# A decoder step on one Trainium2 core: the last two row tiles of the output projections multiplied together, and the rows behind them transposed in two halves

## The chip, the core and the metric

The kernel runs on one core of a Trainium2 chip. A core has TensorE for matmuls (PE in the profile), VectorE (DVE), ScalarE (ACT), GpSimd (POOL), SyncE (SP, which issues most transfers) and 16 DMA engines. Each engine takes its own instructions in order and waits for the others through semaphores. The metric is the device time of one execution in microseconds; lower is better.

## The reference

One layer of a decoder for a prompt of 1024 rows and for a group of 8 sample rows, all in float32. Only this part of it bears on the change:

```python
xp = xp + merge_heads(fox_prompt(q, k, v, logf), sgu_prompt(u, z, w_s[l], b_s[l]),
                      g_att_out[l], g_sgu_out[l], w_o[l])        # ... @ w_o, 1024 x 1024
...
xp = xp + cross_attend(rmsnorm(xp, g_cross[l]), mk, mv, w_cq[l], w_co[l])
f, conv_p = conv_ffn(rmsnorm(xp, g_ffn[l]), zeros, w_up[l], conv_w[l], conv_b[l], w_down[l])
xp = xp + f

def rmsnorm(x, g):
    return x * rsqrt(mean(x * x, axis=-1) + EPS) * g
def cross_attend(xn, mk, mv, w_cq, w_co):
    q = (xn @ w_cq)...   # then softmax over 256 memory rows
    return o @ w_co
```

So there are two output projections (w_o and w_co). Behind each stands a residual add, a norm of the sum, and a projection of the normed rows (w_cq, and the up projection of the feed-forward part). The sample rows go through the same layer, with attention over 8192 cached keys and values each, read page by page from a paged cache.

## The kernel before, in words

The prompt is worked in two halves of 512 rows, and a half is four tiles of 128 rows (tiles 0 to 3). Products of float32 are made in three terms: each operand is split into a high part in a short float format and a remainder, and one 128-row slice of the contraction takes three matmuls, high by high, high by low and low by high (`gemm3`, L270 to L272). The split of an operand is one pass on ACT (the high part, L236, or L233 for weights) and one on DVE (the remainder, L237, or L234). A contraction of 1024 has 8 slices, so one output tile of 128x512 takes 24 matmuls.

`out_proj` is called four times: for w_o and for w_co in each half. It works the 1024 output columns in two parts. In the first (n = 0) all four row tiles are multiplied slice by slice together. In the second (n = 1) the tiles are multiplied one after the other, 24 matmuls each, and each is followed by `residual` (L960 adds the product to the rows in place on DVE; L228 squares and sums them on ACT). Tile 3's residual of the second part is put in at high priority. Where the feed-forward part follows (w_co, `ys` given), the rows are also scaled by their norm factor: `factor` (L976 on ACT, then a power on POOL, L977) and `scaled` (L983 on ACT), tile 3's in two halves of 512 columns and only once the transposing has got to it.

`norm_T` stands behind each `out_proj`: behind w_o at the head of `cross`, behind w_co at the head of `ffn`. It turns the rows around by matmuls against the identity (transposes), splits them, and feeds the first output tile of the next projection as they come (`first`). It takes tiles 0 to 2 together first: eight PSUM banks with three transposes each (L1035), a split of 384 columns each, then 24 matmuls of 384 columns. Tile 3 follows: 8 transposes (L1051), eight splits of 128 columns, 24 matmuls of 128 columns. The other output tiles of the next projection take all 512 columns at once and come behind that.

The places of this text are numbered by time: place 1 is w_o and the cross norm of the first half, place 2 w_co and the feed-forward norm of the first half, places 3 and 4 the same of the second half.

The sample rows run as a background: a generator whose steps are put between those of the prompt at a given pace and which `held[0]` stops from the end of an `out_proj` to the end of the `norm_T` behind it. Its DVE work is large passes over cache pages: L1346 (keys times query) and L1350 (sum), some 1.2 us each for 128x1024. What is issued here is then ordered for each engine by a scheduler that plans with estimated durations and priorities; an engine follows its list in order. PSUM has four banks of pool `ba` and two of `bb` that the products and the transposes share. The split weights have five buffers for the high part (`wh`) and four for the remainder (`wl`).

## Time and profile before

| what | value |
|---|---|
| median of 3 runs | 1874.36 us (1873.6 to 1876.26) |
| profiled execution, its own time | 1871.72 us |
| its span in the trace | 1870.0 us |
| granted TensorE clock, mean | 0.983 |
| PE / DVE / ACT / POOL busy | 95% / 74% / 40% / 27% |

The busy share says which engine carries the span; the chain of work that ended last says who was waited for, step by step. In a table of windows each engine has its busy time and the count of its instructions in the stretch, then the clock that TensorE was granted (1.00 is full), the busy share of the DMA engines and the rate. A row of the timeline has the start, the duration, engine, line, operation and tiles, and in square brackets how long the engine had been idle and for whom it waited. A row of the waits has the waiting engine, line and tile, who released it, the total, the count and the longest. The duration of one matmul includes its way through the array, so matmuls overlap: how fast they follow each other is read from their starts.

### The profile page before, as it was taken

The numbers are of one execution on the slowest core, as the hardware profiler recorded it, in microseconds if no ns is written. First come the engines' busy times: TensorE is split into PE (matmuls) and PEld (weight loads), VectorE is DVE, ScalarE is ACT, GpSimd is POOL, SyncE is SP. The second block draws the span as 40 slices with busy tenths as digits, with TensorE's granted clock in tenths as the row PEclk, the third lists the DMA queues.
The fourth block names the chain that finished last, engine by engine and source line by source line (L and its number), as shares of the span: only waits on it lengthen the run. The fifth ranks groups of instructions, "written<-read, shape, count | busy, mean of one in ns | idle before, by whom it ended". The sixth has DMA issues, their size and how long they took to land.

```text
span 1870.0 us, 24215 instructions
## 1 busy us (share of the span) xinstructions
PE 1785.5 (95%) x9239; PEld 1296.8 (69%) x9239; DVE 1391.7 (74%) x1664; ACT 749.3 (40%) x1363; POOL 497.9 (27%) x437
## 2 busy tenths in 40 slices
PE   8999998788998999999999999989899999999998
PEld 5987666556676767776777776766576668767775
DVE  4889568776778787889989899898875549754344
ACT  6332355565633445433323234234354333333232
POOL 1232352241121322214233242343222112111110
PEclk9999999998999999999999999999999999999999
DMA  8877889684596867668878789888787678578972
GB/s 316 295 260 274 312 303 325 226 247 141 193 396 230 336 244 289 240 245 328 313 264 314 286 316 357 351 305 339 294 306 288 253 258 287 172 264 270 346 287 80
DMA packets 157012, 521.27 MB, mean 279 GB/s; under 512 B 20808, under 2 KB 40520, under 8 KB 124128
## 3 DMA queue, kind: packets, MB, share of 16 engines
q0 software_dynamic: 57168, 341.14, 49.0%
q1 hardware_dynamic: 92816, 165.99, 25.5%
q10 hardware_dynamic: 6912, 12.59, 1.8%
q8 instruction: 73, 1.20, 0.3%
q14 instruction: 43, 0.35, 0.0%
HBM read 495.73 MB, written 23.93 MB: 278 GB/s over the span
## 4 chain that ended last, share of the span: by engine, by line
PE 72%; issue 9%; DVE 7%; DMA 6%; ACT 3%; POOL 3%; SPq 0%; POOLq 0%; DVEq 0%; ACTq 0%
PE ba L270 11%; PE ba L272 11%; PE ba L271 10%; PE bb L270 6%; PE bb L271 6%; PE bb L272 6%; PE dv L1405 5%; DMA kv<-cache_k,kidx 3%; DVE s L1350 2%; DMA kv<-cache_v,kidx 1%; DVE kv L1346 1%; PE ba L1001 1%; PE dv L1669 1%; PE ba L1002 1%; PE ba L1003 1%
## 5 line engine op out<-in xcount | busy, mean ns | idle before, releaser
L233 ACT ACTIVATE wh<-wr 128x1024 fp32r<-128x1024 f32 (+2 forms) x220 | 228.6, 1044 | 501.6 <-PE ba L271 159.7
L234 DVE TENSOR_TENSOR wl<-wr,wh 128x1024 fp32r<-128x1024 f32 (+2 forms) x220 | 262.6, 1201 | 154.0 <-PE ba L272 58.2
L1340 POOL DMA_INDIRECT kv<-cache_k,kidx x128 | 198.5, 1551 | 616.8 <-DVE s L1350 403.9
L1346 DVE TENSOR_TENSOR kv<-kv,d 128x1024 f32<-128x1024 f32 (+1 forms) x184 | 295.5, 1635 | 37.1 <-DMA kv<-cache_k,kidx 28.0
L1350 DVE TENSOR_REDUCE s<-kv 128x16 f32<-128x1024 f32 (+1 forms) x184 | 296.6, 1627 | 0.1
L1399 POOL DMA_INDIRECT kv<-cache_v,kidx x128 | 173.7, 1357 | 294.0 <-PE dv L1405 216.8
L270 PE MATMUL ba<-wh,u 128*128 128x512 f32 (+1 forms) x601 | 229.3, 383 | 5.6 <-DVE u L960 2.7
L271 PE MATMUL ba<-wl,u 128*128 128x512 f32 (+1 forms) x601 | 228.1, 380 | 0.0
L272 PE MATMUL ba<-wh,u 128*128 128x512 f32 (+1 forms) x601 | 225.1, 380 | 0.0
L271 PE MATMUL ba<-u,wh 128*128 128x512 f32 (+2 forms) x520 | 202.7, 390 | 1.3 <-DVE u L237 1.3
L270 PE MATMUL ba<-u,wh 128*128 128x512 f32 (+2 forms) x520 | 202.3, 391 | 0.0
L272 PE MATMUL ba<-u,wl 128*128 128x512 f32 (+2 forms) x520 | 201.9, 389 | 0.0
L270 PEld LDWEIGHTS ba<-wh,u 128*128 128x128 f32 x601 | 113.2, 189 | 36.8 <-issue 8.0
L270 PE MATMUL bb<-u,wh 128*128 128x512 f32 (+2 forms) x344 | 136.6, 397 | 0.0
L1405 PE MATMUL dv<-kv,s 128*32 128x512 f32 x1024 | 131.2, 617 | 5.3 <-DMA kv<-cache_v,kidx 5.3
L271 PE MATMUL bb<-u,wh 128*128 128x512 f32 (+2 forms) x344 | 136.0, 395 | 0.2 <-DVE u L237 0.2
L272 PE MATMUL bb<-u,wl 128*128 128x512 f32 (+2 forms) x344 | 135.3, 394 | 0.0
L272 PEld LDWEIGHTS ba<-wh,u 128*128 128x128 f32 x601 | 113.0, 188 | 27.5 <-issue 6.1
L271 PEld LDWEIGHTS ba<-wl,u 128*128 128x128 f32 x601 | 113.3, 189 | 25.6 <-issue 4.8
L271 PEld LDWEIGHTS ba<-u,wh 128*128 128x128 f32 x520 | 98.6, 190 | 29.7 <-issue 7.2
L272 PEld LDWEIGHTS ba<-u,wl 128*128 128x128 f32 x520 | 98.2, 189 | 27.4 <-issue 7.6
L270 PEld LDWEIGHTS ba<-u,wh 128*128 128x128 f32 x520 | 98.2, 189 | 25.1 <-issue 4.6
(427 smaller groups left out, 3040.8 us busy)
## 6 DMA issues: line engine op xcount, KB each, us to landing
wr<-w_up SPq DMA_DIRECT2D x88, 512.0 KB
kv<-w_up POOLq DMA_DIRECT2D x22, 1024.0 KB, 7.8
wr<-w_down SPq DMA_DIRECT2D x40, 512.0 KB
kv<-w_down POOLq DMA_DIRECT2D x11, 1024.0 KB, 6.2
wr<-w_in SPq DMA_DIRECT2D x16, 512.0 KB
wr<-w_o SPq DMA_DIRECT2D x16, 512.0 KB
wr<-w_cq SPq DMA_DIRECT2D x16, 512.0 KB
wr<-w_co SPq DMA_DIRECT2D x16, 512.0 KB
```

What stands on the lines that cost most here:

```text
L233: nc.scalar.activation(h, src, AF.Copy)
L234: nc.vector.tensor_tensor(l, src, h.bitcast(F32), op=ALU.subtract)
L270: mmul(out, sh, mh, start=(i == 0), stop=False)
L271: mmul(out, sh, ml, start=False, stop=False)
L272: mmul(out, sl, mh, start=False, stop=(i == n - 1))
L1001: mmul(pss[i], mh[k][:, tb], wh, start=(k == korder[0]), stop=False)
L1002: mmul(pss[i], mh[k][:, tb], wl, start=False, stop=False)
L1340: nc.gpsimd.indirect_dma_start(kv, None, a["cache_k"], off(kidx[:, b, ch : ch + 1]))
L1346: nc.vector.tensor_tensor(kvv[:, i : i + m, :], kvv[:, i : i + m, :], qb.unsqueeze(1).broadcast_to((P, m, 512)), op=ALU.mult)
L1350: nc.vector.tensor_reduce(s[:, ch * 4 + i : ch * 4 + i + m, :].rearrange("p k h -> p (k h)"), kvv[:, i : i + m, :].rearrange("p k (h d) -> ...
L1399: nc.gpsimd.indirect_dma_start(kv, None, a["cache_v"], off(kidx[:, b, ch : ch + 1]))
L1405: mmul(dv[32 * j : 32 * j + 32, :], s[:, ch * 4 : ch * 4 + 4, :].rearrange("p k h -> p (k h)"), kvv[:, j, :], start=(ch == 1), stop=(ch == ...
```

## The change

In the second column part of `out_proj`, tiles 0 and 1 are multiplied as before, and tiles 2 and 3 as a pair: each slice of the weights is used for both before the next. The residuals of both tiles then follow the pair, both at high priority. With `ys`, tiles 0 and 1 are scaled at full width, and tiles 2 and 3 later, in alternating halves of 512 columns (`both`). `norm_T` takes tiles 0 and 1 first and then tiles 2 and 3, with the same code: for each half four PSUM banks of four transposes, eight splits of 256 columns, and 24 matmuls of 256 columns.

```diff
@@ residual @@
-        with tc.high_priority() if HP and i == 3 and n == 1 else nullcontext():
+        with tc.high_priority() if HP and i > 1 and n == 1 else nullcontext():
@@ out_proj @@
         def scaled(i, r):
             y = U([P, D])
-            for c in (slice(0, 512), slice(512, D)) if i == 3 else (slice(0, D),):
-                nc.scalar.activation(y[:, c], xt[i][:, c], AF.Copy, scale=r)
+            nc.scalar.activation(y, xt[i], AF.Copy, scale=r)
             return y
+        def both(r2, r3):
+            y2, y3 = U([P, D]), U([P, D])
+            for c in (slice(0, 512), slice(512, D)):
+                nc.scalar.activation(y2[:, c], xt[2][:, c], AF.Copy, scale=r2)
+                nc.scalar.activation(y3[:, c], xt[3][:, c], AF.Copy, scale=r3)
+            return [y2, y3]
...
-            for i in range(4):          # n == 1: one tile, gemm3 over 8 slices, then its residual
-                    ps = MM()
-                    gemm3(ps[:, :512], [... for k in korder])
-                if ys is not None and n == 1 and i > 0:
-                    ys.append(scaled(i - 1, factor(i - 1)))
-                residual(xt, sq, i, n, ps)
-                held[0] = n == 1 and i == 3
-                yield 5.2 if n else 0.1
+            for group in ((0,), (1,), (2, 3)):
+                pss = [MM() for _ in group]
+                for k in korder:
+                    wh, wl = (ws[k // 2][q][:, k % 2, :] for q in range(2))
+                    for i, ps in zip(group, pss):
+                        tb = slice(i * P, (i + 1) * P)
+                        mmul(ps, mh[k][:, tb], wh, start=(k == korder[0]), stop=False)
+                        mmul(ps, mh[k][:, tb], wl, start=False, stop=False)
+                        mmul(ps, ml[k][:, tb], wh, start=False, stop=(k == korder[-1]))
+                    if len(group) == 2 and k == korder[3]:
+                        yield 5.2
+                if ys is not None and group[0]:
+                    ys.append(scaled(group[0] - 1, factor(group[0] - 1)))
+                for i, ps in zip(group, pss):
+                    residual(xt, sq, i, n, ps)
+                held[0] = len(group) == 2
+                yield 5.2
         if ys is not None:
             with tc.high_priority():
-                ys.append(partial(scaled, 3, factor(3)))
+                ys.append(partial(both, factor(2), factor(3)))
@@ norm_T @@
-        for kk in range(8):             # tiles 0 to 2: 3 transposes, split of 384
-            ...
-        first(hs, ls, slice(0, 384))
-        yield 4
-        for k4 in range(0, 8, 4):       # tile 3: 4 transposes a bank, splits of 128
-            ...
-        first(hs, ls, slice(384, 512))
+        for t0 in (0, 2):
+            c = slice(t0 * P, (t0 + 2) * P)
+            if callable(ys[t0]):
+                ys[t0:] = ys[t0]()
+            for kk in range(0, 8, 2):
+                ...
+                tr = TR()               # 2 slices x 2 tiles = 4 transposes
+                ...
+                for q in range(2):
+                    k = kk + q
+                    split(tr[:, q * 256 : (q + 1) * 256], hs[k][:, c], ls[k][:, c], scale=gp[:, g0 + k : g0 + k + 1])
+                yield 0.6
+            first(hs, ls, c)
+            if t0 == 0:
+                yield 3
```

Up to the first second-part product of w_o the order of every engine is the same. PE has 6942 rows before and 6946 now, DVE 1491 and 1484, ACT 1169 and 1171; POOL (442) and SP (408) keep their counts. Lines behind the edit move by 14 (the key passes L1346 and L1350 are L1360 and L1364 after it).

On PE at place 1, before, tile 3's product (into `ba_4974`, the row tiles' slices are `u`) ends and the transposes (L1035) of tiles 0, 1 and 2 begin:

```order
L272 MATMUL ba_4974<-wh_4858,u_4631 128x512
L270 MATMUL ba_4974<-wh_4858,u_4630 128x512
L271 MATMUL ba_4974<-wl_4857,u_4630 128x512
L272 MATMUL ba_4974<-wh_4858,u_4631 128x512
L1035 MATMUL ba_5035<-cp,u_4678 128x128
L1035 MATMUL ba_5035<-cp,u_4680 128x128
L1035 MATMUL ba_5035<-cp,u_4682 128x128
L1035 MATMUL ba_5043<-cp,u_4678 128x128
```

Now, with tiles 2 and 3 in `ba_4931` and `ba_4932` taking turns at each slice and the transposes being L1059:

```order
L1028 MATMUL ba_4932<-wh_4858,u_4631 128x512
L1026 MATMUL ba_4931<-wh_4858,u_4630 128x512
L1027 MATMUL ba_4931<-wl_4857,u_4630 128x512
L1028 MATMUL ba_4931<-wh_4858,u_4631 128x512
L1026 MATMUL ba_4932<-wh_4858,u_4630 128x512
L1027 MATMUL ba_4932<-wl_4857,u_4630 128x512
L1028 MATMUL ba_4932<-wh_4858,u_4631 128x512
L1059 MATMUL ba_5037<-cp,u_4678 128x128
L1059 MATMUL ba_5037<-cp,u_4680 128x128
L1059 MATMUL ba_5037<-cp,u_4678 128x128
L1059 MATMUL ba_5037<-cp,u_4680 128x128
```

The transposes that follow the product read tiles 0 and 1 (`u_4678`, `u_4680`) alone.

On DVE at the same place, before, from tile 1's residual (L960) to the first remainder of the transposed rows (L237); `wl` are the remainders of w_cq's slices, L1346 and L1350 the background:

```order
L960 TENSOR_TENSOR u_4680<-bb_4903,u_4680 128x512
L960 TENSOR_TENSOR u_4682<-ba_4931,u_4682 128x512
L1332 TENSOR_TENSOR dec_4968<-ms_4965,d_1004_4806 128x512
L234 TENSOR_TENSOR wl_5012<-wr_5010,wh_5013 128x1024
L1346 TENSOR_TENSOR kv_4959<-kv_4959,d_388_2409 128x1024 x2
L234 TENSOR_TENSOR wl_5018<-wr_5016,wh_5019 128x1024
L1350 TENSOR_REDUCE s_2411<-kv_4959 128x16
L234 TENSOR_TENSOR wl_5024<-wr_5022,wh_5025 128x1024
L1350 TENSOR_REDUCE s_2411<-kv_4959 128x16
L234 TENSOR_TENSOR wl_5030<-wr_5028,wh_5031 128x1024
L960 TENSOR_TENSOR u_4684<-ba_4974,u_4684 128x512
L237 SCALAR_TENSOR_TENSOR u_5040<-ba_5035,gp,u_5039 128x384
```

Now (L1346 is what L1332 was, L1360 and L1364 the key passes):

```order
L960 TENSOR_TENSOR u_4680<-bb_4903,u_4680 128x512
L234 TENSOR_TENSOR wl_5012<-wr_5010,wh_5013 128x1024
L234 TENSOR_TENSOR wl_5018<-wr_5016,wh_5019 128x1024
L1346 TENSOR_TENSOR dec_4966<-ms_4963,d_1004_4806 128x512
L1360 TENSOR_TENSOR kv_4957<-kv_4957,d_388_2409 128x1024 x2
L234 TENSOR_TENSOR wl_5024<-wr_5022,wh_5025 128x1024
L1364 TENSOR_REDUCE s_2411<-kv_4957 128x16 x2
L960 TENSOR_TENSOR u_4682<-ba_4931,u_4682 128x512
L234 TENSOR_TENSOR wl_5030<-wr_5028,wh_5031 128x1024
L960 TENSOR_TENSOR u_4684<-ba_4932,u_4684 128x512
L237 SCALAR_TENSOR_TENSOR u_5036<-ba_5037,gp,u_5035 128x256
```

Tile 2's residual has moved behind three of the four `wl` passes and both key passes, tile 3's stays last, and two `wl` passes have moved to the front.

On ACT at place 2, before, behind the last weight split there, to the first high part of tile 3 (L236 high parts, L228 squares, L976 factors, L983 scaling; `u_4684` is tile 3):

```order
L236 ACTIVATE u_6251<-ba_6255,gp 128x384
L236 ACTIVATE u_6265<-ba_6269,gp 128x384
L228 ACTIVATE junk_6208,sqx_5831<-u_4684 128x512
L236 ACTIVATE u_6265<-bb_6261,gp 128x384
L976 ACTIVATE fac_1272_6210<-sqx_5831,part_5832 128x1
L228 ACTIVATE junk_6213,ssu_5054<-u_5740 128x512
L228 ACTIVATE junk_6215,ssu_5054<-u_5740 128x512
L236 ACTIVATE u_6279<-ba_6275,gp 128x384
L236 ACTIVATE u_6279<-bb_6283,gp 128x384
L983 ACTIVATE u_6289<-u_4684,fac_1272_6210 128x512 x2
L236 ACTIVATE u_6237<-ba_6316,gp 128x128
```

Now, from tile 2's factor to the first high part of the second half (L989 and L990 scale tiles 2 and 3, `u_4682` and `u_4684`):

```order
L976 ACTIVATE fac_1268_6203<-sqx_5829,part_5830 128x1
L228 ACTIVATE junk_6201,sqx_5829<-u_4684 128x512
L236 ACTIVATE u_6229<-bb_6231,gp 128x256
L236 ACTIVATE u_6240<-ba_6242,gp 128x256
L976 ACTIVATE fac_1269_6206<-sqx_5829,part_5830 128x1
L228 ACTIVATE junk_6209,ssu_5051<-u_5738 128x512
L236 ACTIVATE u_6251<-ba_6253,gp 128x256
L989 ACTIVATE u_6297<-u_4682,fac_1268_6203 128x512 x2
L236 ACTIVATE u_6262<-bb_6264,gp 128x256
L228 ACTIVATE junk_6211,ssu_5051<-u_5738 128x512
L990 ACTIVATE u_6298<-u_4684,fac_1269_6206 128x512 x2
L236 ACTIVATE u_6229<-ba_6303,gp 128x256
```

Before, one tile's square, factor and scaling stand among the splits; now there are those of two (tile 2's square is a few rows further up), and the scaling of tile 2 stands ahead of the last split of the first half.

On DVE at place 3, before, among the last remainders of tile 3:

```order
L237 SCALAR_TENSOR_TENSOR u_9882<-ba_9942,gp,u_9881 128x128
L1085 TENSOR_SCALAR rq_9984<-rn0r_9981 128x4
L237 SCALAR_TENSOR_TENSOR u_9868<-ba_9929,gp,u_9867 128x128
L1346 TENSOR_TENSOR kv_9730<-kv_9730,d_1660_8597 128x1024 x2
L237 SCALAR_TENSOR_TENSOR u_9896<-ba_9942,gp,u_9895 128x128
L1350 TENSOR_REDUCE s_8599<-kv_9730 128x16
L237 SCALAR_TENSOR_TENSOR u_9868<-ba_9929,gp,u_9867 128x128
L1350 TENSOR_REDUCE s_8599<-kv_9730 128x16
L1346 TENSOR_TENSOR kv_9775<-kv_9775,d_1660_8597 128x1024 x2
L237 SCALAR_TENSOR_TENSOR u_9896<-ba_9942,gp,u_9895 128x128
```

Now, among those of the second half:

```order
L1364 TENSOR_REDUCE s_8596<-kv_9596 128x16
L237 SCALAR_TENSOR_TENSOR u_9871<-ba_9934,gp,u_9870 128x256
L1364 TENSOR_REDUCE s_8596<-kv_9596 128x16
L237 SCALAR_TENSOR_TENSOR u_9860<-bb_9925,gp,u_9859 128x256
L237 SCALAR_TENSOR_TENSOR u_9882<-ba_9943,gp,u_9881 128x256
L1360 TENSOR_TENSOR kv_9686<-kv_9686,d_1656_8594 128x1024 x2
L237 SCALAR_TENSOR_TENSOR u_9871<-ba_9934,gp,u_9870 128x256
L237 SCALAR_TENSOR_TENSOR u_9860<-bb_9925,gp,u_9859 128x256
L237 SCALAR_TENSOR_TENSOR u_9882<-ba_9943,gp,u_9881 128x256
L1364 TENSOR_REDUCE s_8596<-kv_9686 128x16 x2
L234 TENSOR_TENSOR wl_10138<-wr_10136,wh_10139 128x1024
L1360 TENSOR_TENSOR kv_9729<-kv_9729,d_1656_8594 128x1024 x2
```

The key passes over `kv_9730` stood between tile 3's remainders; the passes over that page (`kv_9729` now) stand behind all of them.

44 lines of the change are left out of this document (16 added, 28 removed).

## The prediction

> **What bounds the kernel now.** I read the page first, for the busy shares and the chain that ended last:
>
> ```profile
> PE 1785.5 (95%) x9239; PEld 1296.8 (69%) x9239; DVE 1391.7 (74%) x1664; ACT 749.3 (40%) x1363; POOL 497.9 (27%) x437
> ...
> PE 72%; issue 9%; DVE 7%; DMA 6%; ACT 3%; POOL 3%; SPq 0%; POOLq 0%; DVEq 0%; ACTq 0%
> ```
>
> TensorE carries the span, and 7% of the chain is DVE. So an edit can win by less TensorE time or by shorter waits of TensorE. The change touches four places (w_o and w_co in each half, numbered as above). Next I read what TensorE waited for from the end of the product to the end of the transposed block, places 1 to 4 in this order:
>
> ```profile
> PE ba L1035 <- DVE u L960: 3.9, 1, 3.9
> PE ba L606 <- issue: 1.9, 1, 1.9
> ...
> PE bb L1035 <- DVE u L960: 2.5, 1, 2.5
> PE ba L1035 <- DVE u L237: 1.1, 1, 1.1
> ...
> PE ba L1051 <- DVE u L237: 3.7, 3, 1.6
> PE ba L271 <- DVE u L237: 1.3, 2, 1.1
> ...
> PE bb L1035 <- DVE u L960: 0.2, 1, 0.2
> ```
>
> That is 5.8, 3.6, 5.0 and 0.2 us, nearly 15 us in all, 0.8% of the span. DVE is named nearly always, by tile 3's residual (L960, which frees a PSUM bank that the transposes need) or by a remainder (L237). Place 4 hardly waits. Third, stretches of those places; the last but two columns hold the granted clock:
>
> ```profile
> 572.00:574.00 2.00, 2.00 (x10) 1.98 (x11) 2.00 (x5) 1.97 (x4) 0.17 (x1) 0.50 1.01 375
> ...
> 582.00:584.00 2.00, 2.00 (x10) 1.82 (x10) 2.00 (x3) 0.50 (x2) 0.00 (x0) 0.50 0.00 0
> ...
> 739.00:741.00 2.00, 2.00 (x9) 1.95 (x8) 2.00 (x5) 1.97 (x7) 0.55 (x1) 0.50 1.02 408
> ...
> 1228.00:1232.00 4.00, 3.17 (x16) 2.67 (x16) 4.00 (x7) 0.50 (x2) 0.00 (x0) 1.00 1.00 417
> ```
>
> Behind the long waits of places 1 and 2 TensorE works for some 3 us at half its clock, which costs about 1.6 us each time. At place 3 the waits are shorter pieces and the clock stays full.
>
> **The change part by part: TensorE's own work.** Transposes stay 32 a place. The 24 matmuls of 384 columns and 24 of 128 become 48 of 256. Place 4 shows the first two undisturbed (first and last of 21, first and last of 10), and a run of 96 of 260 columns early in the program is the nearest row to 256:
>
> ```profile
> 1392.44 0.33 PE L271 MATMUL ba<-u,wh 128*128 128x384 f32 x1
> ...
> 1395.94 0.34 PE L270 MATMUL ba<-u,wh 128*128 128x384 f32 x1
> ...
> 1403.90 0.27 PE L272 MATMUL ba<-u,wl 128*128 128x128 f32 x1
> ...
> 1404.90 0.27 PE L272 MATMUL ba<-u,wl 128*128 128x128 f32 x1
> ...
> 61.27 0.39 PE L270 MATMUL ba<-wh,u 128*128 128x260 f32 x1
> ...
> 72.77 0.28 PE L272 MATMUL ba<-wh,u 128*128 128x260 f32 x1
> ```
>
> Start to start: 3.50/20 = 0.175 us, 1.00/9 = 0.111 us, 11.50/95 = 0.121 us (0.119 for 256 columns in proportion). A matmul of 128 columns costs nearly as much as one of 256. So 24 x (0.175 + 0.111) = 6.9 us become 48 x 0.119 = 5.7 us, 1.2 us less a place, 4.7 us over four. It counts only where TensorE isn't waiting for DVE or ACT anyway.
>
> The Trainium skill, "TensorE: Matmul & The Clock Gate", section "Back-to-back issue gap", gives the isolated gap as columns/2.4 + 2.5 ns; by it 128 columns take 56 ns, 256 take 109 and 384 take 163, and the change saves nothing (5.2 us either way), which would make the sum below 2.4 us worse (places 3 and 4). The measured 0.111 us speaks against that formula here; the page itself says that it undercounts at small sizes.
>
> The splits, before:
>
> ```profile
> L236 ACT ACTIVATE u<-ba,gp 128x384 fp32r<-128x384 f32 x21 | 11.3, 580 | 2.3 <-PE ba L1035 2.3
> L236 ACT ACTIVATE u<-ba,gp 128x128 fp32r<-128x128 f32 x28 | 10.3, 368 | 35.8 <-PE ba L1051 35.7
> ...
> L237 DVE SCALAR_TENSOR_TENSOR u<-ba,gp,u 128x384 fp32r<-128x384 f32 x21 | 12.3, 614 | 0.0
> L237 DVE SCALAR_TENSOR_TENSOR u<-ba,gp,u 128x128 fp32r<-128x128 f32 x28 | 9.7, 352 | 12.9 <-ACT u L236 12.8
> ...
> L983 ACT ACTIVATE u<-u,fac 128x1024 f32<-128x1024 f32 x6 | 6.9, 1149 | 4.0 <-POOL fac L977 4.0
> ```
>
> A split of 256 has no row; by the mean of 384 and 128 it is 474 ns on ACT and 483 on DVE. Eight and eight of them are what eight of 384 and eight of 128 were, so neither engine gets more or less; only the order counts.
>
> **Place 1.** On DVE before, from tile 1's residual to the first remainder, and tile 3's product on TensorE, its first and last matmul:
>
> ```profile
> 556.07 0.67 DVE L960 TENSOR_TENSOR u<-bb,u 128x512 f32<-128x512 f32 x1
> 560.34 0.69 DVE L960 TENSOR_TENSOR u<-ba,u 128x512 f32<-128x512 f32 x1 [3.60 <-PE ba L272]
> ...
> 562.18 1.23 DVE L234 TENSOR_TENSOR wl<-wr,wh 128x1024 fp32r<-128x1024 f32 x1 [0.17 <-issue]
> ...
> 571.26 0.69 DVE L960 TENSOR_TENSOR u<-ba,u 128x512 f32<-128x512 f32 x1
> 571.86 1.14 DVE L237 SCALAR_TENSOR_TENSOR u<-ba,gp,u 128x384 fp32r<-128x384 f32 x2
> ...
> 560.66 0.50 PE L270 MATMUL ba<-wh,u 128*128 128x512 f32 x1
> ...
> 566.08 0.39 PE L272 MATMUL ba<-wh,u 128*128 128x512 f32 x1
> ```
>
> DVE stands still for 3.60 us until tile 2's product is there, then works without a gap to 571.86, over 5 us past the product's end. That backlog is what TensorE waits for. The first w_cq remainder waits until w_o's first slices are read for the last time, inside tile 3's product. With the pair, which takes the 11 us of both, they are read out a quarter of the way, at about 557.5 instead of 562. As the order shows, two remainder passes (1.2 us each) now stand ahead of tile 2's residual; the first falls into the idle 3.60 us, the second starts at about 560.3, when the second slices are out. The rest of the list is the same work, so the first L237 comes 1.2 us less a little reordering earlier: -1.1 us. TensorE's own saving is worth nothing here, since DVE is behind; that cover would be gone only if DVE caught up. Ends: 0 (the background's keys arrive late and hold the list) to -2.8 (the wait gets short enough for full clock, another 1.6).
>
> **Place 2.** ACT before, and TensorE at the end of the product and at the end of the 384-column block:
>
> ```profile
> 735.34 1.06 ACT L233 ACTIVATE wh<-wr 128x1024 fp32r<-128x1024 f32 x1 [0.28 <-DMA wr<-w_up]
> 736.31 1.51 ACT L236 ACTIVATE u<-ba,gp 128x384 fp32r<-128x384 f32 x3
> 737.70 0.63 ACT L228 ACTIVATE junk<-u 128x512 bf16<-128x512 f32 x1
> ...
> 741.28 1.33 ACT L983 ACTIVATE u<-u,fac 128x512 f32<-128x512 f32 x2
> ...
> 732.37 0.40 PE L272 MATMUL bb<-wh,u 128*128 128x512 f32 x1
> ...
> 745.23 0.22 PE L270 MATMUL ba<-u,wh 128*128 128x128 f32 x1
> ```
>
> Tile 2's square, factor and scaling used to be done before the product ended; now they come behind it, with tile 3's. The transfer that releases the weight split at 735.34 doesn't move, so ACT goes on at 736.3. By the new order there follow five splits (0.38 each start to start, a little under their duration), two factors (0.2), three squares with their reads (0.7), tile 2's scaling (1.33) and half of tile 3's (0.7): 6.4 us, to 742.7. Then the remaining transposes (1.5), the first split (0.5) and 24 x 0.119 = 2.9: 747.6. Before, 745.23 plus tile 3's six remaining transposes (0.7) and its 24 x 0.111 = 2.7: 748.6. That is -1.0, and I add 0.6 because TensorE idles 5 us of these 10 and may be throttled later, when it has work (0.4 of 1.6): -0.4 us. Ends: -2.0 (no throttling) to +3.0 (the second half stands still for the whole scaling of two tiles).
>
> The page and section on the clock gate in the same Trainium skill page, "Part 1: The HAM clock gate", put the drop behind an idle window of about 3.4 us. The 0.50 at 572 behind 3.9 us agrees; the one at 739, behind waits of 2.5 and 1.1 us with work between them, says that less is enough here. If only a wait over 3.4 us did it, place 2 would be throttled no longer, and the sum would be 1.6 us better.
>
> **Place 3.** DVE before, and POOL at place 2:
>
> ```profile
> 1240.84 2.36 DVE L1346 TENSOR_TENSOR kv<-kv,d 128x1024 f32<-128x1024 f32 x2 [1.64 <-DMA kv<-cache_k,kidx]
> ...
> 735.36 1.71 POOL L1340 DMA_INDIRECT kv<-cache_k,kidx  x1 [5.40 <-DVE s L1350]
> ```
>
> This key pass waits 1.64 us for its page while two of tile 3's remainders stand behind it in DVE's list. In the new order all remainders of the second half come ahead of that page; fewer key passes are mixed among them, and the background's work comes later, where the products of 512 columns cover it. I count two waits left, about 2.0 us for the first half's remainders and 1.5 in the second: 3.5 for 5.0, so -1.5, and the saved 1.2 of TensorE counts too: -2.7 us. Ends: 0 (another page holds the list) to -5.0 (no wait left).
>
> **Place 4.** There is no wait to win: 0.2 us. Behind the product ACT now has eight splits (3.8), two squares with reads (1.6), two factors (0.6) and the scaling in four halves (2.8), 8.8 us; TensorE has 32 transposes (3.5, at the 0.111 of a 128-column matmul) and half of the matmuls (2.9), 6.4 us, ahead of tile 3's last slices. The difference, 2.4, and the wait for the first factor's power on POOL (0.5) make 2.85 of idle, less the 1.2 saved: +1.65 us. Ends: 0 (the splits overlap) to +3.0.
>
> **Queues.** On POOL at place 2, tile 2's factor now stands behind the key transfer of 735.36, which waits for DVE; it ends at 737.1, and by the ACT order tile 2's factor isn't asked for before that. At place 4 both factors stand behind three value transfers that end, before, ahead of the product's end. SP's list has a few loads of w_cq and w_co a place or two earlier or later; nothing reads them within 5 us. I take 0 for these.
>
> **Sum.** -1.1 - 0.4 - 2.7 + 1.65 = -2.55 us on the profiled execution (1871.72): 1869.2. That execution lies 2.6 us under the median of 1874.36, so the median should be about 1871.8. The ends add up to -9.8 and +6.0.
>
> **Rivals.** What a measurement of this kernel can tell from no change is about 0.2%, 3.7 us.
>
> *Faster: the clock stays full.* If the shorter waits of places 1 and 2 throttle TensorE no longer, 1.6 us is won three times on top (572, 582 and 739): -7.4, 1867.0. For it: at place 3 pieces up to 1.6 us left the clock at 1.00. Against: at place 1 nearly 3 us of waiting remains. A smaller place 4 term (0 for 1.65) or no wait left at place 3 leads to the same side.
>
> *Slower: two tiles' scaling behind the product.* At places 2 and 4 the second half can't be transposed until ACT has squared, factored and scaled two tiles, and nothing else is in TensorE's order between the halves. If ACT's list is held once more by a weight load or POOL's factor by a page transfer, each place pays its +3.0 and one throttling of 1.6: +9.2, less 1.1 and 2.7 at the others: +5.4, 1879.8. It decides from about 4 us of idle more at the two places together than I count. For it: place 2 already waits for w_up at 735.34. Against: the full clock and 0.2 us at place 4 show how much slack ACT had there.
>
> *No change: DVE bound.* Places 1 and 3 end when DVE has done its list, whatever TensorE saves: 0 there and 1.2 lost again at place 4, about 1875. This lies in the forecast's own case. That the change isn't carried out as written is excluded by the order.
>
> **Chances.** Within 0.2% (the forecast, -2.55 being 0.14%): 0.39. Faster, by the clock or by larger terms: 0.37. Slower by the scaling: 0.24. The range reaches nearly to both ends: 1865 to 1880.
>
> **What would show it.** In the changed profile: the first L237 of place 1 near 570.7 and its wait on L960 near 3 us; two remainder passes ahead of tile 2's residual, the first in DVE's old gap; 256-column matmuls 0.12 us apart; at place 3 no wait for a key page among the remainders and 3 to 4 us of idle; at places 2 and 4 a wait of the L1059 transposes for ACT's L989 or L990. I am wrong if that wait is over 4 us, if the granted clock stays at 1.00 through places 1 and 2, or if time is won or lost outside the four places, where the order is reshuffled too.

## The result

The changed kernel takes 1864.71 us (median of 9 runs, 1857.88 to 1869.87) where the kernel before takes 1873.6 us in the runs beside them (9 runs, 1870.61 to 1879.34): a ratio of 0.9944, interval 0.9930 to 0.9957. That is 0.56% faster. The forecast was 1871.8 us, "within 0.2%", with a range from 1865 to 1880: both the case and the range missed, the range by 0.3 us.

The profiled execution of the changed kernel took 1858.95 us, span 1857.2 us, which is 5.8 us under its median, where that of before lay 2.6 us under its own. So traces compared directly overstate the gain by about 3 us. The page of the changed kernel, busy shares and chain:

```profile
PE 1779.9 (96%) x9239; PEld 1290.3 (69%) x9239; DVE 1390.5 (75%) x1666; ACT 749.2 (40%) x1365; POOL 488.5 (26%) x437
...
PE 67%; DVE 10%; issue 9%; DMA 9%; ACT 4%; POOL 2%; SPq 0%; POOLq 0%; DVEq 0%; ACTq 0%
```

TensorE is busy 5.6 us less with the same 9239 instructions; DVE and ACT do what they did.

What TensorE waits for behind the product at places 1 to 4, largest rows of each, in the same view as before the change (line, releaser, us in total, times, longest):

```profile
PE ba L606 <- issue: 2.0, 1, 2.0
PE ba L1059 <- DVE u L960: 1.9, 2, 1.1
PE bb L271 <- DVE u L237: 0.5, 1, 0.5
...
PE bb L1059 <- DVE u L960: 2.2, 1, 2.2
PE ba L271 <- DVE u L237: 2.0, 3, 1.4
...
PE ba L1059 <- DVE u L960: 1.8, 2, 1.1
PE bb L271 <- DVE u L237: 1.2, 1, 1.2
PE ba L1106 <- issue: 1.1, 1, 1.1
...
PE ba L270 <- ACT u L236: 0.8, 2, 0.5
```

These rows hold 4.4, 4.2, 4.1 and 0.8 us, where those of before held 5.8, 3.6, 5.0 and 0.2. DVE is still the engine that is waited for most at places 1 to 3, now in shorter pieces: the longest wait for it is 1.1 us for 3.9, 2.2 for 2.5 and 1.2 for 1.6. (At place 1 the 2.0 us before L606, for which the profile names no releaser, stood there before as well, with 1.9.) In sum place 2 waits longer than before. The clock behind these waits, places 1 and 2 (start and end, length, busy time of PE, PEld, DVE, ACT, POOL, granted clock, DMA share, GB/s):

```profile
570.00:572.00 2.00, 2.00 (x12) 2.00 (x10) 2.00 (x2) 0.47 (x1) 0.00 (x0) 0.50 1.00 413
580.00:582.00 2.00, 2.00 (x10) 1.70 (x8) 2.00 (x5) 0.00 (x0) 0.00 (x0) 0.50 0.57 234
...
730.00:732.00 2.00, 0.84 (x3) 0.55 (x3) 2.00 (x6) 2.00 (x7) 0.56 (x1) 0.50 0.99 348
734.00:736.00 2.00, 2.00 (x11) 2.00 (x11) 0.65 (x2) 2.00 (x6) 0.10 (x1) 0.50 0.75 303
```

The clock is halved at both places, as before: shorter single waits did not keep it full.

Where the time went is seen best by cutting every trace at TensorE's own landmarks: A runs from the start to the first w_o matmul of half 1; 1 from there to the first transpose of place 2; 2 to the second half's w_o; 3 to the first transpose of place 4; 4 to the last matmul. So place 1 lies in part 1, place 2 at the head of part 2, place 3 in part 3, place 4 at the head of part 4. In us, means of two traces of each kernel (the second pair is in the first experiment):

| part | before | changed | difference | forecast |
|---|---|---|---|---|
| A, up to place 1 | 516.5 | 512.0 | -4.5 | 0 |
| 1, with place 1 | 216.3 | 213.4 | -2.9 | -1.1 |
| 2, with place 2 | 438.6 | 434.6 | -4.0 | -0.4 |
| 3, with place 3 | 218.2 | 215.6 | -2.7 | -2.7 |
| 4, with place 4 | 474.4 | 475.9 | +1.5 | +1.65 |
| sum | 1864.0 | 1851.5 | -12.5 | -2.55 |

The surplus is in A, where nothing was changed, in part 1, and in part 2. The two last parts came out near the forecast, but the two traces of one kernel lie 1.8 to 3.2 us apart there, so agreement to a tenth is luck. Differences are taken before rounding. These four traces overstate the gain: 12.5 us, where the medians give 8.9.

### The profile page after: what moved, and what is told of

It is laid out like the page before. It is cut to its first block, busy times and chain, and to the rows that moved or that the text cites. A ratio compares the mean times of both kernels' runs of the same rounds, so it can differ in the third digit from the quotient of the medians.

```text
span 1857.2 us, 24238 instructions
## 1 busy us (share of the span) xinstructions
PE 1779.9 (96%) x9239; PEld 1290.3 (69%) x9239; DVE 1390.5 (75%) x1666; ACT 749.2 (40%) x1365; POOL 488.5 (26%) x437
## 4 chain that ended last, share of the span: by engine, by line
PE 67%; DVE 10%; issue 9%; DMA 9%; ACT 4%; POOL 2%; SPq 0%; POOLq 0%; DVEq 0%; ACTq 0%
PE ba L270 9%; PE ba L271 9%; PE ba L272 9%; PE dv L1419 5%; PE bb L271 5%; PE bb L270 4%; PE bb L272 4%; DMA kv<-cache_v,kidx 2%; DVE kv L1360 2%; DMA kv<-cache_k,kidx 2%; DVE s L1364 2%; PE ba L1008 1%; DVE wl L234 1%; PE ba L1010 1%; PE ba L1009 1%
## 5 line engine op out<-in xcount | busy, mean ns | idle before, releaser
L1354 POOL DMA_INDIRECT kv<-cache_k,kidx x128 | 185.3, 1448 | 611.5 <-DVE s L1364 376.6
L1360 DVE TENSOR_TENSOR kv<-kv,d 128x1024 f32<-128x1024 f32 (+1 forms) x185 | 295.6, 1628 | 42.6 <-DMA kv<-cache_k,kidx 42.5
L1364 DVE TENSOR_REDUCE s<-kv 128x16 f32<-128x1024 f32 (+1 forms) x185 | 295.9, 1619 | 0.1
L271 PE MATMUL ba<-u,wh 128*128 128x512 f32 (+1 forms) x560 | 220.6, 394 | 2.3 <-DVE u L237 2.1
L270 PE MATMUL ba<-u,wh 128*128 128x512 f32 (+1 forms) x560 | 219.8, 394 | 1.3 <-ACT u L236 1.1
L272 PE MATMUL ba<-u,wl 128*128 128x512 f32 (+1 forms) x560 | 219.7, 393 | 0.0
L270 PE MATMUL ba<-wh,u 128*128 128x512 f32 (+1 forms) x495 | 185.6, 378 | 1.4 <-DVE u L740 1.0
L271 PE MATMUL ba<-wl,u 128*128 128x512 f32 (+1 forms) x495 | 186.3, 377 | 0.0
L272 PE MATMUL ba<-wh,u 128*128 128x512 f32 (+1 forms) x495 | 184.2, 376 | 0.0
L270 PEld LDWEIGHTS ba<-u,wh 128*128 128x128 f32 x560 | 106.0, 190 | 33.8 <-issue 9.3
L271 PEld LDWEIGHTS ba<-u,wh 128*128 128x128 f32 x560 | 106.4, 190 | 33.1 <-issue 7.1
L271 PE MATMUL bb<-u,wh 128*128 128x512 f32 (+1 forms) x304 | 118.2, 389 | 1.7 <-DVE u L237 1.7
L270 PE MATMUL bb<-u,wh 128*128 128x512 f32 (+1 forms) x304 | 118.0, 389 | 0.5 <-ACT u L236 0.5
L272 PE MATMUL bb<-u,wl 128*128 128x512 f32 (+1 forms) x304 | 116.8, 384 | 0.0
L270 PEld LDWEIGHTS ba<-wh,u 128*128 128x128 f32 x495 | 92.9, 188 | 26.5 <-issue 5.9
L271 PEld LDWEIGHTS ba<-wl,u 128*128 128x128 f32 x495 | 93.1, 188 | 22.2 <-issue 5.9
L272 PEld LDWEIGHTS ba<-wh,u 128*128 128x128 f32 x495 | 93.1, 188 | 19.9 <-issue 3.1
## 6 DMA issues: line engine op xcount, KB each, us to landing
wr<-w_up SPq DMA_DIRECT2D x88, 512.0 KB
wr<-w_down SPq DMA_DIRECT2D x40, 512.0 KB
wr<-w_in SPq DMA_DIRECT2D x16, 512.0 KB
wr<-w_o SPq DMA_DIRECT2D x16, 512.0 KB
wr<-w_cq SPq DMA_DIRECT2D x16, 512.0 KB
wr<-w_co SPq DMA_DIRECT2D x16, 512.0 KB
```

What stands on the lines that cost most here:

```text
L270: mmul(out, sh, mh, start=(i == 0), stop=False)
L271: mmul(out, sh, ml, start=False, stop=False)
L272: mmul(out, sl, mh, start=False, stop=(i == n - 1))
L1354: nc.gpsimd.indirect_dma_start(kv, None, a["cache_k"], off(kidx[:, b, ch : ch + 1]))
L1360: nc.vector.tensor_tensor(kvv[:, i : i + m, :], kvv[:, i : i + m, :], qb.unsqueeze(1).broadcast_to((P, m, 512)), op=ALU.mult)
L1364: nc.vector.tensor_reduce(s[:, ch * 4 + i : ch * 4 + i + m, :].rearrange("p k h -> p (k h)"), kvv[:, i : i + m, :].rearrange("p k (h d) -> ...
```

## The experiments

Every kernel was timed in 5 rounds against the kernel before on the same chip. Ratios stand with their intervals.

**The two kernels once more.** First the noise: the changed kernel and the kernel before, each run again with no edit.

> The changed kernel once more, unaltered, for a second trace. Theory A (the gain is made at the four places: shorter waits behind the products, TensorE's own 4.7 us) expects the ratio 0.994 again and, in the trace, the transposed blocks of places 1 to 4 shorter together by about 8 us. Theory B (the places give some 3.5 us, and the rest comes from what the new order moved behind them, such as TensorE's waits near 1166 and 1311 us, which the first trace has shorter) expects the same time, with waits of places 1 to 4 as in the first trace and again 4 to 5 us gained outside them. If the two traces differ there by more than 3 us, single traces can't settle it.

> The kernel before once more, for a second trace. The ratio is 1.000. It tells whether the 3 to 4 us by which both traces of the changed kernel are ahead before the first changed instruction (DVE waits 0.6 to 1.3 us instead of 4.5 for a transfer of cq_d near 355 us) are chance: if this trace has the short wait too, they are; if it has the long one again, as the other kernels' traces have, the changed program wins them by something that the orders don't show.

Measured: the changed kernel 1864.25 us, 0.9955 (0.994 to 0.997); before against itself 1874.15 us, 1.0005 (0.9991 to 1.002). At this pace of the background the gain is real, and about 0.5%. A second trace of each also tells what is scatter. For the transposed block (the product's end to the last 256- or 128-column matmul), the length times what its mean clock is short of 1 is 3.4 and 1.7 us at place 1 in the two traces of the changed kernel, and 0 and 3.4 us at place 3 in the two of before. The order of instructions is the same within each pair. So a place has no fixed loss to the clock. Without their products of 512 columns and the background's the four blocks take together 64.6 and 64.4 us in the changed kernel, for 68.1 and 72.1: 3.5 to 7.7 us less, between what the two theories had.

**One edit without the other.** The pair alone, with three tiles and then one transposed as before:

```diff
-            if ys is not None:
-                ys.append(partial(both, factor(2), factor(3)))
+                ys.append(scaled(2, factor(2)))
+                ys.append(partial(scaled, 3, factor(3)))
...
     def norm_T(ys, g0, first):
-        (two halves of two tiles)
+        (three tiles, then one, as before)
```

> The pair and the priority of tile 2's residual, but the transposing of three tiles and then one as before. Theory A: DVE gets to the remainders at places 1 and 3 earlier (1 to 3 us each), but no TensorE work is saved and the first block of three tiles now waits for tile 2, which is ready only at the end of the pair: within 3 us of before, 0.999 to 1.002. Theory B: the pair alone moves the loads and the background too, so it could keep about half of the gain, 0.997.

And the halves alone, with tiles 2 and 3 multiplied one behind the other:

```diff
-            for group in ((0,), (1,), (2, 3)):
+            for group in ((0,), (1,), (2,), (3,)):
...
-        with tc.high_priority() if HP and i > 1 and n == 1 else nullcontext():
+        with tc.high_priority() if HP and i == 3 and n == 1 else nullcontext():
```

> The two halves of two tiles, but the output projections' tiles one after the other as before (tiles 2 and 3 are scaled late, in alternating halves). Theory A: TensorE's 1.2 us a place are saved wherever it isn't waiting, and the first half needs no late tile: 0.996 to 0.998. Theory B: no telling by the places, the saving of 4.7 us is not reached: 0.999.

Measured: pair alone 1882.52 us, 1.0054 (1.0040 to 1.0069); halves alone 1878.46 us, 1.0038 (1.0020 to 1.0056). Neither theory had this: at this one phase of the background each half of the change loses by itself, and together they win. (How much of it is the clock is told below.) The waits name a reason at the places. Pair alone, places 2 and 4 (transposes for the scaling of a tile), then halves alone, place 1:

```profile
PE ba L1065 <- ACT u L993: 2.2, 1, 2.2
...
PE ba L1065 <- ACT u L993: 1.6, 1, 1.6
...
PE ba L1107 <- DVE u L966: 3.7, 1, 3.7
```

With the pair alone, tile 2 is finished as late as tile 3, but the first transposes need it: they wait for its scaling. With the halves alone the first block needs only tiles 0 and 1, but DVE's list is as late as before (3.7 us, for 3.9). The pair makes room in DVE's list, and the halves make the late tile 2 harmless. Part 2 and part 4, which begin with those two places, take 3.4 and 3.9 us more with the pair alone (442.0 and 478.3). With the halves alone it is part 4 that loses, 4.5 us (478.9); 1.5 us of it lie in the block at place 4 (13.3 us for 11.8), and what the rest is stays open. At place 1 the block takes, without its products of 512 columns, 23.3 us before, 22.9 and 23.0 us with one edit, 19.9 and 19.6 us with both.

**The priority alone.** The changed kernel also marks tile 2's residual as urgent:

```diff
-        with tc.high_priority() if HP and i == 3 and n == 1 else nullcontext():
+        with tc.high_priority() if HP and i > 1 and n == 1 else nullcontext():
```

> The kernel before with only the priority: tile 2's residual at high priority too (in the output projections and in the last group of the feed-forward part). The prediction gave this no time of its own: 1.000. If the scheduler's reshuffle by itself moves the time, it is off by over 0.2% to either side.

Measured: 1872.65 us, 1.0004 (0.9988 to 1.0021): no difference at this pace, as expected.

**By place.** The whole change at w_o alone, at w_co alone, and everywhere but at place 4:

```diff
+        paired = two = place in (1, 3)       # w_o alone
+        paired = two = place in (2, 4)       # w_co alone
+        paired = two = place in (1, 2, 3)    # not place 4
```

> The whole change at places 1 and 3 (w_o) alone, the kernel before at places 2 and 4. The prediction's terms give -1.1 and -2.7, 3.8 us: 0.998. The first trace, by the length of the transposed blocks less the 512-column products in them, gives -3.4 and -1.8, 5.2 us: 0.997. Theory B adds what is moved behind these places: 0.995.

> The whole change at places 2 and 4 (w_co) alone, the kernel before at places 1 and 3. The prediction's terms: -0.4 and +1.65, that is 1.0007. By the two traces of the changed kernel, from the w_co product's end to the next place: place 2 with the feed-forward part behind it -3.3 and -4.4, place 4 with the rest +1.5 and +3.3, so about -1.5 us, 0.999. If it is under 0.997, w_co carries the gain and w_o (0.9984 alone) does not.

> The whole change at places 1, 2 and 3, the kernel before at place 4. If place 4 costs 1.5 to 3.3 us, as the two traces and the prediction (+1.65) have it, this is 1.5 to 3 us faster than the changed kernel: 0.993 to 0.994. If the cost belongs to the background that is left for the end, and not to place 4, it stays at 0.995.

Measured: w_o alone 1869.8 us, 0.9984 (0.9973 to 0.9995); w_co alone 1866.34 us, 0.9961 (0.9941 to 0.9980); without place 4 1867.2 us, 0.9977 (0.9961 to 0.9993). The two sets add up to the whole, within their intervals: -0.16% and -0.39% for -0.56%. w_o alone came as forecast; the other two missed what was expected. The larger share came from w_co, where the forecast had +1.25 us, and leaving out place 4, which it charged with 1.65 us, made the kernel no faster. By part, w_co alone wins 5.0 us in part 2 (433.6 for 438.6) and 4.0 in part 3 (214.3 for 218.2), where it changes nothing. And w_o alone moves 11.3 us out of part 3 (206.9 for 218.2) and 9.6 us into part 4 (484.0 for 474.4).

Part 2 shows where. The time lost in it runs alike before and after up to about its 1500th product; the difference falls at the end of the first feed-forward part, some 400 us behind place 2. TensorE's waits there and DVE's list, before (L1350 is a key sum, L960 the residual that frees the PSUM bank):

```profile
PE ba L270 <- DVE u L960: 2.7, 2, 2.5
...
1162.95 2.26 DVE L1350 TENSOR_REDUCE s<-kv 128x32 f32<-128x2048 f32 x1
1165.12 0.68 DVE L960 TENSOR_TENSOR u<-ba,u 128x512 f32<-128x512 f32 x1
```

and after (the key sum is L1364):

```profile
PE ba L270 <- DVE u L960: 0.3, 1, 0.3
...
1155.08 0.67 DVE L960 TENSOR_TENSOR u<-ba,u 128x512 f32<-128x512 f32 x1
1156.33 2.27 DVE L1364 TENSOR_REDUCE s<-kv 128x32 f32<-128x2048 f32 x1
```

Before, the residual for which TensorE waits stood right behind a key sum of 2.26 us, and the waits came to 2.7 us; now the next key sum comes behind the residual, and the wait is 0.3 us. Beyond its products (0.231 us each, 0.115 for those of the background) the end of part 2, from its 1410th product on, costs 5.9 us in both traces of the changed kernel, and 10.4 and 9.1 in those of before. Halves alone, w_co alone and "not place 4" have 5.9, 6.8 and 5.9 there. The priority, which reaches the residuals of the feed-forward part too, isn't it: alone it has 10.6. It is the background, the key passes that are dealt out between TensorE's steps, that has come out in another phase; the next experiments move nothing else.

**Another phase of the background.** So how much of the 0.5% belongs to the edit, and how much to the phase in which the background happens to stand? The pace numbers that deal it out were moved by little, with and without the change:

```diff
-PACE = {..., 'ffn0': 8.5, 'att1': 15.0, 'mid1': 6.8, ...}
+PACE = {..., 'ffn0': 8.4, 'att1': 15.0, 'mid1': 6.8, ...}    # or 8.6
+PACE = {..., 'ffn0': 8.5, 'att1': 15.0, 'mid1': 6.9, ...}
```

> The kernel before, with nothing changed but the background's pace in the first half's feed-forward part (8.4 for 8.5). In its order one key pass stands between the last residuals of that part where two stood, and 11 key passes among the remainders of place 3 where 14 stood. Theory P (much of the gain is where the background's passes happen to fall: 4 us at the end of the first feed-forward part, some of the 5 at place 3) expects 3 to 6 us faster, 0.997 to 0.998. Theory L (the gain is made by the pair and the halves themselves) expects 1.000.

> The same with 8.6 for 8.5. One pass between the residuals, 12 among the remainders of place 3. Theory P: 2 to 5 us faster, 0.997 to 0.999. Theory L: 1.000.

> The changed kernel with the pace of 8.6. Among the remainders of places 1 and 3 stand 6 and 8 key passes as without it, but a pass falls between the last residuals of the first feed-forward part. Theory P: 2 to 4 us of the gain are lost, 0.997. Theory L: the gain stays, 0.995.

> The changed kernel with the background's pace of the first feed-forward part at 8.4 (the kernel before with 8.4 took 1.0022). Theory L (the change wins about 3 us at each of the places 1 to 3, wherever the background falls, and the rest of a time is the background's phase): in the trace, places 1 to 3 with what follows them are together 8 to 14 us shorter than with 8.4 before, and the time is 0.995 to 0.998. Theory P (the gain belongs to the one phase that 8.5 has): within 0.2% of 1.0022.

> The kernel before with the background's pace between the second half's w_o and its feed-forward part at 6.9 (6.8 before). Nothing ahead of place 3 is moved; 14 key passes stay among the remainders of place 3. The pair to the next kernel: 0.998 to 1.003, by the phase in which the background reaches place 4.

> The changed kernel with the pace of 6.9 there. Theory L: 6 to 10 us under the kernel before with 6.9, as places 1 to 3 keep their gain (0.994 to 0.998). Theory P: the difference to it is under 3 us. If ACT waits over 3 us for the load of w_up at place 4, as in the two slow variants of the changed kernel, that place gives back 3 to 7 us.

Measured, as ratios to the kernel before:

| pace | without the change | with it | the change's worth |
|---|---|---|---|
| as it is | 1.0005 (0.9991 to 1.0020) | 0.9955 (0.9940 to 0.9970) | -0.50% |
| ffn0 8.4 | 1.0022 (1.0006 to 1.0038) | 0.9995 (0.9980 to 1.0010) | -0.27% |
| ffn0 8.6 | 0.9996 (0.9974 to 1.0017) | 0.9992 (0.9977 to 1.0008) | -0.04% |
| mid1 6.9 | 1.0001 (0.9989 to 1.0014) | 1.0031 (1.0016 to 1.0046) | +0.30% |

The same edit is worth anything from -0.5% to +0.3%, by one step of a pace that it doesn't touch. Neither theory survives: L's number came true for the kernel before at 8.6 alone. The range for the kernel before at 6.9 held, and the remark on ACT's load at place 4; the other numbers missed. The mean of the four is -0.13%, about 2.4 us; each worth is uncertain by about 0.2%, so that mean is a sign of the size and no more. Over the four paces the changed kernel itself moves by 0.76% (0.9955 to 1.0031), the kernel before by 0.26%.

**Where the change keeps its gain and where it loses it.** The blocks at the places themselves, without products and background, in us (with the pace as it is, two traces; otherwise one trace each; without the change, then with it):

| pace | place 1 | place 2 | place 3 | place 4 |
|---|---|---|---|---|
| as it is | 23.3, 23.3; 19.9, 19.6 | 15.8, 16.5; 17.2, 17.2 | 17.2, 20.3; 15.4, 15.4 | 11.8, 11.9; 12.1, 12.2 |
| ffn0 8.4 | 23.3; 19.1 | 15.9; 17.2 | 16.2; 14.7 | 14.5; 11.1 |
| ffn0 8.6 | 24.1; 19.1 | 16.6; 17.3 | 19.1; 16.5 | 14.8; 18.1 |
| mid1 6.9 | 23.3; 19.1 | 15.8; 17.3 | 17.4; 15.4 | 12.7; 18.4 |

So places 1 and 3 win and place 2 loses at every pace: that is the edit. Place 4 goes either way, and the kernel before, too, takes 11.8 to 14.8 us there. At 8.6 and 6.9 the changed kernel loses at place 4 (part 4 takes 5.5 and 13.1 us more than without the change). At 8.4 it loses at the end of the first feed-forward part, where it had won: the end of part 2 costs 11.5 us beyond its products, for 7.1 without the change, and TensorE waits for a remainder (L240):

```profile
PE ba L273 <- DVE u L240: 3.8, 1, 3.8
```

(Single traces can lie far from the medians, up to 10 us for the kernel before at 8.6, so parts of traces don't add up to the table of ratios.) With mid1 at 6.9 part 4 takes 486.8 us, where the changed kernel has 475.0 and 476.8 and the kernel before at this pace 473.7. The waits of the changed kernel there at 6.9, then ACT's at 8.6 (part 4: 483.8 us) and ACT's row in "not place 4", which has place 4 as before (L236 is the weight split in all three kernels, L239 the split of rows, L999 the scaling of tile 2, L1107 the transposes):

```profile
PE ba L273 <- ACT u L239: 2.7, 2, 1.8
PE bb L1107 <- ACT u L999: 2.1, 1, 2.1
ACT wh L236 <- DMA wr<-w_up: 3.8, 1, 3.8
...
ACT wh L236 <- DMA wr<-w_up: 4.9, 1, 4.9
...
1376.51 1.06 ACT L236 ACTIVATE wh<-wr 128x1024 fp32r<-128x1024 f32 x1 [4.20 <-DMA wr<-w_up]
```

ACT stands 3.8 to 4.9 us before a weight split whose load hasn't landed, with the splits and the scaling that TensorE needs queued behind it. At mid1 6.9 the block at place 4 then takes the 18.4 us of the table, for 12.1. In the changed kernel as it is, the same split waits for TensorE instead, until the product is about done, and little behind it is late (ACT at place 4; the first row's wait, 3.76 us, is for a matmul of the product):

```profile
1374.31 1.06 ACT L233 ACTIVATE wh<-wr 128x1024 fp32r<-128x1024 f32 x1 [3.76 <-PE bb L1028]
...
1379.37 0.74 ACT L989 ACTIVATE u<-u,fac 128x512 f32<-128x512 f32 x1
...
1381.21 0.73 ACT L990 ACTIVATE u<-u,fac 128x512 f32<-128x512 f32 x1
1381.83 0.48 ACT L236 ACTIVATE u<-ba,gp 128x256 fp32r<-128x256 f32 x1
```

**The clock in every execution.** Each execution's mean granted clock is on record, so its span can be divided: what the clock is short of 1, times the span, is the most that the halved clock can have cost (TensorE is idle in part of it), and the rest is the time apart from the clock. Means over the executions in us, the differences uncertain by about 2:

| pace | halved clock, without and with | difference | rest, without and with | difference |
|---|---|---|---|---|
| as it is | 31.4, 29.8 | -1.6 | 1840.2, 1832.5 | -7.7 |
| ffn0 8.4 | 32.2, 36.1 | +4.0 | 1840.9, 1832.2 | -8.7 |
| ffn0 8.6 | 29.0, 33.6 | +4.6 | 1841.6, 1834.6 | -6.9 |
| mid1 6.9 | 29.8, 35.6 | +5.8 | 1839.8, 1837.8 | -1.9 |

Apart from the clock the change is worth 6.3 us on the mean, and 7 to 9 at three of the four paces; at the same time the clock takes back 4 to 6 us wherever the pace was moved. In the traces 3.4 us of that lie at place 4 at 8.6 and 6.9, behind ACT's wait, and 5.1 in part 2 at 8.4. Divided in the same way, the pair alone loses 8.9 us to the clock and only 1.8 apart from it, the halves alone 5.0 and 2.7; w_o alone wins 6.2 us apart from the clock and loses 3.7 to it, w_co alone wins 4.0 and 2.6. So the larger share of w_co above is the clock's, and apart from it w_o has the larger one.

**Holding the background back.** If fewer background passes among the remainders are what helps at places 1 and 3, holding them from the start of the second column part should help the kernel before as well:

```diff
+            held[0] = place in (1, 3)
             for i in range(4):
...
-                held[0] = n == 1 and i == 3
+                held[0] = i == 3 or place in (1, 3)
```

> The kernel before, with the background held back already from the start of w_o's second column part (places 1 and 3). In its order 10 key passes stand among the remainders of place 3 where 14 stood, and 8 at place 1 as before. If a pass among the remainders costs what it takes (1.2 us), place 3 ends some 4 to 5 us earlier, and the time is 0.998, unless the background that is held back is missed at the end; if the passes are hidden, 1.000.

Measured: 1884.0 us, 1.0073 (1.0042 to 1.0104), outside both expectations. Part 1 takes 227.6 us for 216.3, part 3 208.5 for 218.2. The block at place 1 is as long as before (23.1 us for 23.3, with the same 8 passes), so part 1 loses behind it, on the way to the next product (96.5 us for 83.1 and 81.6), probably where what was held back is done; in part 3 holding back paid. The edit did not thin out the passes at place 1, so it says nothing on what they cost there.

## Why the prediction was right or wrong

**Place 1: the term was too small, -1.1 for -2.9.** The order was read rightly. DVE on the changed kernel's trace:

```profile
551.74 0.67 DVE L960 TENSOR_TENSOR u<-bb,u 128x512 f32<-128x512 f32 x1
553.06 1.23 DVE L234 TENSOR_TENSOR wl<-wr,wh 128x1024 fp32r<-128x1024 f32 x1 [0.65 <-issue]
555.82 1.22 DVE L234 TENSOR_TENSOR wl<-wr,wh 128x1024 fp32r<-128x1024 f32 x1 [1.53 <-PE ba L1027]
...
563.61 0.68 DVE L960 TENSOR_TENSOR u<-ba,u 128x512 f32<-128x512 f32 x1
565.34 0.69 DVE L960 TENSOR_TENSOR u<-ba,u 128x512 f32<-128x512 f32 x1
565.94 0.87 DVE L237 SCALAR_TENSOR_TENSOR u<-ba,gp,u 128x256 fp32r<-128x256 f32 x2
...
582.14 0.48 DVE L237 SCALAR_TENSOR_TENSOR u<-bb,gp,u 128x256 fp32r<-128x256 f32 x1
```

The first remainder pass stands in the old gap, 8.9 us ahead of the product's end (561.97), and DVE's 3.60 us of standing still became 0.65 and 1.53. The first L237 starts 3.97 us behind the product's end, where it was 5.55 us before (the forecast: 4.4). The step that failed is the next sentence, "TensorE's own saving is worth nothing here, since DVE is behind". In the block, the time that is neither waiting nor lost to the clock fell from 13.0 us to 11.6 and 11.9, and TensorE's idle time from 7.0 to 4.9 and 6.0: the saving counted. The account that fits is that the wait isn't one wait for the end of DVE's list but several for its items, with matmuls between them. And DVE's list got shorter where it matters. Before, the last remainder of place 1 was this one:

```profile
592.35 0.34 DVE L237 SCALAR_TENSOR_TENSOR u<-bb,gp,u 128x128 fp32r<-128x128 f32 x1
```

That is 26.0 us behind the product's end; now it is 20.2 us (582.14), with 7.3 us of background among the remainders instead of 11.6. The forecast looked at the first remainder and not at the last. The block is shorter by 3.4 to 5.0 us at all four paces, so this is the edit and not the phase.

**Place 2: -0.4 forecast, +1.0 at the place, and the gain elsewhere.** The block takes 17.2 us in both traces, for 15.8 and 16.5: the second half did wait (idle 4.5 and 4.1 us for 3.6 and 3.2; 3.4 us to the clock in both, for 1.7 and 3.4), inside the ends of -2.0 and +3.0. The predicted wait for the scaling (L989, L990) is not among the rows: it is DVE's residual, 2.2 us, and a remainder, 1.4. Part 2 is still 4.0 us shorter, by the residual at the end of the feed-forward part shown above. No term of the sum lay there: it put everything outside the four places at nothing, and that is its second failed step. The prediction's last sentence named this as the way to be wrong: "time is won or lost outside the four places, where the order is reshuffled too".

**Place 3: right in its mechanism, with luck in the number.** By part it is -2.7 for -2.7; the block itself takes 15.4 us in both traces, for 17.2 and 20.3, and the 3.4 us between these two are the clock. (That the clock stays full there, as the prediction read it, held for one trace of before and not for the other.) TensorE idles 4.3 and 3.1 us (forecast 3 to 4), and no remainder waits for a key page. But w_co alone, which leaves place 3 as it was, also wins 4.0 us in part 3.

**Place 4: right by total, +1.5 for +1.65, not by its working.** The block costs 0.3 us more (12.1 and 12.2 for 11.8 and 11.9), the rest lies behind it, and at the other paces the place costs anything from -3.4 to +5.7 us. TensorE idles 1.1 us, not 2.85: ACT's splits of 256 follow each other by 0.36 us, where the mean of 384 and 128 gave 0.474, so ACT keeps up.

**TensorE's own work: right.** Matmuls of 256 columns at place 4, the first and the last of 14:

```profile
1389.11 0.28 PE L271 MATMUL ba<-u,wh 128*128 128x256 f32 x1
...
1390.64 0.28 PE L272 MATMUL ba<-u,wl 128*128 128x256 f32 x1
```

Start to start 1.53/13 = 0.118 us, where 0.119 was read off the row of 260 columns.

**The rivals.** "The clock stays full" gave 1867.0 us, the nearest number, by a mechanism that didn't happen: the clock is halved at places 1 and 2. Its price per throttling, 1.6 us, was right (1.7); what it took as fixed, and what isn't, is how many of them a place has, as the pairs of identical kernels show. The rule tried beside place 2, that only a wait over 3.4 us throttles, fails: no wait there before, and none at places 1 and 2 now, is longer than 2.5 us, and the clock was halved. "Two tiles' scaling behind the product" did not happen in the changed kernel, but it is real: its trigger, "if ACT's list is held once more by a weight load", is what the paces 8.6 and 6.9 show at place 4, with 6.3 us more in the block at 6.9; at 8.6 the kernel before, too, waits 1.9 us for the scaling there. "DVE bound" fell with place 1, where TensorE's saving counted.

**What the sum left out** is the phase of the background, and with it the clock. The prediction priced four places against one trace in which the key passes stand as they do; an edit that changes the number or length of steps deals them out anew, as the end of part 2 shows some 400 us later. That the mean worth over four paces, -0.13%, is about the forecast (-0.14%) is luck: it is 6.3 us won apart from the clock, where the forecast had about 3, less some 3 us that the clock takes. The range should have held both: the changed kernel moves by 0.76% over the four paces, about 14 us; its lower end was set from the places alone.

**Part A stays open.** Some 3.7 of its 4.5 us are one wait (0.67 us and none in the two traces of the changed kernel, for 3.87 and 4.15). DVE's L598 reads a loaded operand, some 355 us into the program; before, then changed, then the load in each:

```profile
356.83 2.74 DVE L598 SCALAR_TENSOR_TENSOR u<-u,rz,t 128x512 f32<-128x512 f32 x4 [3.87 <-DMA u<-cq_d]
...
354.18 2.74 DVE L598 SCALAR_TENSOR_TENSOR u<-u,rz,t 128x512 f32<-128x512 f32 x4 [0.67 <-issue]
...
u<-cq_d POOLq DMA_DIRECT2D x2, 8.0 KB, 8.4
...
u<-cq_d POOLq DMA_DIRECT2D x2, 8.0 KB, 4.7
```

The load lands after 4.7 us instead of 8.4. The order of every engine up to there is the same. But the time to landing doesn't decide it alone: at 6.9 it is 6.3 us with the change and a short wait (0.34), and 6.5 without it and a long one (3.33). The short wait shows in three traces, all with the change (both of the changed kernel, and 6.9), and in none of the fourteen others (2.75 to 4.19 us); the changed kernel at 8.4 and 8.6 has the long one. No run tells what decides it.

## What to carry to other kernels

Where background work is dealt out between steps, an edit's worth holds for one phase of it: time the edit at two or three neighbouring paces before keeping or dropping it, and put the spread into the range. Ahead of a forecast, compare the order behind the edited places as well, and look for residuals that free a bank and change places with a long background pass, and, on an engine that works in order, for a load that stands ahead of what TensorE needs. Price a halved clock in whole pieces and leave their number open (here 1.7 us each, and 0 to 2 of them at one place and one order). And before comparing kernels, split each one's time by its granted clock into what the halved clock can have cost and the rest: here that parts a gain of 7 to 9 us at three of four paces from the 4 to 6 us that the clock took back wherever the pace was moved.
